# Block products of layer 0: copied accumulators in one two-bank tile, four weight loads in place of two

## The chip, the cores and the metric

One core of a Trainium2 chip runs the kernel. Its engines have queues of their own: PE (TensorE, matmul; PEld is its weight load), DVE (VectorE), ACT (ScalarE), POOL (GpSimd) and SP (SyncE), which here only issues DMAs. Data lie in SBUF, 128 partitions wide; matmuls write to PSUM, 8 banks of 128 x 512 float32. The metric is the device time of one execution in microseconds (us). Before the change the median of 3 runs was 2519.68 us (2517.79 to 2521.02).

## The reference

One inference step of a two-layer decoder. A prompt of 1024 tokens and 8 single-token samples share all weights, model width 1024. Each layer has a mixer, then a SwiGLU FFN, with norms and a residual around both. Only the FFN matters here:

```python
D_FF = ((8 * D_MODEL + 3 * 256 - 1) // (3 * 256)) * 256      # 2816

def swiglu(h, w_gu, w_down):
    gate, up = jnp.split(h @ w_gu, 2, axis=-1)
    return (jax.nn.silu(gate) * up) @ w_down
```

With `h` of 1024 columns, `h @ w_gu` has 2 x 2816 columns: 22 blocks ("columns", f = 0 to 21) of 128 for the gate and 22 for up.

## The kernel before

**Two groups.** The tokens are worked in two groups, g = 0 with 512 prompt tokens and g = 1 with 512 prompt tokens and the 8 samples (520, as two halves of 260). Everything is transposed: features on the partitions, tokens along the free axis.

**Split matmuls.** Float32 matmuls are made of three `float32r` ones. A raw weight block is copied by ACT to a rounded high part (L259, L561), DVE subtracts that for the low part (L260, L562), and PE multiplies high x high, high x low, low x high into one accumulator. The raw blocks come by DMA on SP into pool `wraw` (5 buffers, tile names w); the split parts lie in `wspl` (5 buffers, ws).

**Block products.** For group 1 some columns of the FFN are made by a seven-product scheme on 2 x 2 blocks in place of eight. The two token halves are one axis of blocks, gate and up another, and the two halves of the 1024 input features the third. A column's weights are four raw blocks of 512 x 128: a11 and a12 are the gate's upper and lower features, a21 and a22 those of up. `sums_here` loads them and gives, for product j, either a raw block or a sum: j = 1 needs a21 + a22, j = 2 needs kept3 = a11 + a21 and kept2 = kept3 + a22, j = 4 uses kept3 and j = 5 needs kept2 + a12. So four DVE sums a column (L536), seven ACT copies (L561) and seven DVE subtractions (L562). The token side's sums are made once by `sums_w` and reused in all columns.

`gate_up_w` runs the seven products (12 matmuls each, 84 a column, L571) on four accumulators. Their order, with what lies between:

- p0 into pa; L578: ACT writes -pa into pb
- p1 into pd; p2 onto pb; L581: ACT writes -pb into pc
- p3 onto pa; L584: silu of pa is one half of the gate
- p4 onto pb; L587: ACT copies pd; L589: DVE adds it to pb
- p5 onto pc; L591: DVE subtracts the copy of pd from pc
- p6 onto pb; L593: silu of the second half; L594 and L595: products of gate and up; then a split to the tile m that w_down reads.

**Where it is used.** Class `ffn` (layer 0) uses it for columns 10 to 21 of group 1: parts 2, 3 and 4 of the FFN in the `PARTS` of 5, 5, 4, 4 and 4 columns. Each part ends with 8 projections by `w_down` (L273) of that part's columns. Its accumulators come from `quads`: two tiles of two banks from pool `mmp` (2 buffers), pa and pd in the first, pb and pc in the second. Its raw blocks are two C tiles of two blocks each (`cpool`, 4 buffers of 128 x 2 x 512). The part before runs beside the stick-breaking and memory attention of group 0, whose last steps (scores L866, softmax, transposes L893, values L907) use the small banks `smp` (3 banks of 512, tile names s). Class `ffn_w` (layer 1) uses it for columns 4 to 21 of group 1, after `mmp` and `smp` were closed: eight single banks, four tags q0 to q3 of two buffers, so pa to pd of two columns have banks of their own. Its first block column (column 4) takes C tiles, later ones A tiles (`apool`, 8 buffers). Column 4 stands beside `store_y`, which transposes the first group's result (L1455), copies it to C tiles (L1458) and stores those (L1460), and beside `token_rows` (L483).

**The order.** The program is recorded by generators that `weave` interleaves by given weights; a scheduler then sets the order of each engine's instructions, and adds the waits, from its own estimates. A tile's buffer is reused when all readers of the tile that had it are done. The order of PE, DVE, ACT and SP below is that of the built program.

Of the kernel before, what the change touches and what calls it, by code (L numbers as in the profile page):

```python
# [8 lines left out]
F32 = mybir.dt.float32  # L9
# [8 lines left out]
P = 128  # L18
# [5 lines left out]
def tile_decoder(  # L24
# [12 lines left out]
    DFF = w_down.shape[1]  # L37
# [10 lines left out]
    def pool(name, bufs, **kw):  # L48
        return ctx.enter_context(tc.tile_pool(name=name, bufs=bufs, **kw))

    const = pool("const", 1)
    wraw = pool("wraw", 5)
    wspl = pool("wspl", 5)
    xpool = pool("xpool", 8)
    apool = pool("apool", 8)
# [8 lines left out]
    mmp = banks.enter_context(tc.tile_pool(name="mmp", bufs=2, space=PSUM))  # L64
# [6 lines left out]
    def nm(s):  # L71
        uid[0] += 1
        return f"{s}_{uid[0]}"
# [12 lines left out]
    def Q(i):  # L86
        return single[0].tile([P, 512], F32, tag=f"q{i}", name=nm("q"))
# [6 lines left out]
    def A(dt=F32):  # L94
        return apool.tile([P, 2, WID], dt, tag="a", name=nm("a"))
# [7 lines left out]
    def R_one():  # L103
        r = rpool.tile([P, ND, WID], F32, tag="r", name=nm("r"))
        return [r[:, k, :] for k in range(ND)]
# [5 lines left out]
    def C():  # L111
        return cpool.tile([P, 2, 512], F32, tag="c", name=nm("c"))

    def S():
        if single:
            turn[0] += 1
            return Q(3 * (turn[0] % 2))
        return smp.tile([P, 512], F32, tag="s", name=nm("s"))

    def small(shape, dt=F32, tag="sm", bufs=None):  # L120
        return spool.tile(shape, dt, tag=tag, name=nm(tag), bufs=bufs)
# [35 lines left out]
    for lv in range(7):  # L157
        m = 1 << lv
# [17 lines left out]
    def gcol(l, i, k):  # L176
        o = (l * 4 + i) * ND + k
        return par[:, o : o + 1]
# [64 lines left out]
    def pv(ps, g):  # L243
        return ps[:, 0, :G] if g == 0 else ps[:, :, : PW[1]]
# [62 lines left out]
    def sq_acc(acc, src, k, n):  # L307
        if k == 0:
            nc.scalar.activation(acc[:, :n], src, AF.Square)
        else:  # L310
            t = N()
            nc.scalar.activation(t[:, :n], src, AF.Square)  # L312
            nc.vector.tensor_add(acc[:, :n], acc[:, :n], t[:, :n])  # L313
# [207 lines left out]
        return mt, last  # L521

    def sums_here(l, f, raws, outs):
        cols = []
        for m0 in (f * P, DFF + f * P):
            r = raws()
            nc.sync.dma_start(
                r.rearrange("p a (k m) -> p (a k) m", m=P), w_gu[l][:, m0 : m0 + P].rearrange("(k p) m -> p k m", p=P)
            )
            cols.append(r)  # L530
        (a11, a12), (a21, a22) = ((r[:, 0, :], r[:, 1, :]) for r in cols)
        kept = {}

        def add(a, b):
            t = outs()
            nc.vector.tensor_add(t, a, b)  # L536
            return t

        def weight(j):
            if j == 1:  # L540
                return add(a21, a22)
            if j == 2:
                kept[3] = add(a11, a21)
                kept[2] = add(kept[3], a22)
                return kept[2]
            if j == 4:
                return kept[3]
            if j == 5:
                return add(kept[2], a12)
            return (a11, None, None, a12, None, None, a22)[j]  # L550

        return weight
# [51 lines left out]
    class ffn_w:  # L604
# [12 lines left out]

        def raws(self):
            if self.pi:
                return apool.tile([P, 2, 512], F32, tag="a", name=nm("w"))  # L620
            return C()

        def part(self, pi):
            l, n, h = self.l, NG[1], PW[1]
            f0, nf = PARTS[pi]
            last = pi == len(PARTS) - 1
            mids = []
            for j in range(nf):
                self.pi = pi
                if f0 + j < self.plain:  # L630
                    mt, ins = gate_up_q(l, f0 + j, self.x)
                    mids.append(mt)
                    with tc.issue_after(ins.ins):
                        for _ in range((1, 2, 1, 0)[j]):
                            next(self.sums, None)
                else:
                    mids.append(gate_up_w(
                        sums_here(l, f0 + j, self.raws, lambda: wraw.tile([P, 512], F32, tag="w", name=nm("w"))),
                        self.ops, self.spl, lambda: [Q(i) for i in range(4)]
                    )[0])  # L640
                yield
            if pi == 0:
                self.R = R_one()
            if last:
                self.acc = small([P, WID], tag="st", bufs=3)
                nc.scalar.preload_act_table_set("natural_log_exp_and_others")
            for m in range(ND):
                w = split_w(w_down[l], f0, nf, m * P)
                pp = [Q(2 * (m % 2) + a) for a in range(2)]
                for k in range(nf):  # L650
                    wh, wl = w[k]
                    for wi, (wt, xi) in enumerate(((wh, 0), (wh, 1), (wl, 0))):
                        for a in range(2):
                            nc.tensor.matmul(  # L654
                                pp[a][:, :h], wt, mids[k][:, xi, a * h : (a + 1) * h],
                                start=(k == 0 and wi == 0), stop=(k == nf - 1 and wi == 2),
                            )
                for a in range(2):
                    d = self.R[m][:, a * h : (a + 1) * h]
                    if pi == 0:  # L660
                        nc.scalar.copy(d, pp[a][:, :h])
                    else:
                        nc.vector.tensor_add(d, d, pp[a][:, :h])
                if last:
                    sq_acc(self.acc, self.R[m][:, :n], m, n)
                    nc.scalar.activation(self.R[m][:, :n], self.R[m][:, :n], AF.Copy, scale=gcol(l, 3, m))
                    if m == 3:
                        first_half(self)
                if m % 2:
                    yield  # L670
# [4 lines left out]
    class ffn:  # L675
        def __init__(self, g, l, xt, rows=False, prod=NF):
# [2 lines left out]
            self.ops = []  # L679
            self.sums = sums_w(xt, self.ops, lambda: A(F32R))  # L680

        def quads(self):
            ta, tb = (mmp.tile([P, 2, 512], F32, tag="mm", name=nm("mm")) for _ in range(2))
            return ta[:, 0, :], tb[:, 0, :], tb[:, 1, :], ta[:, 1, :]

        def part(self, pi):
            g, l = self.g, self.l
            n = NG[g]
            f0, nf = PARTS[pi]
            last = pi == len(PARTS) - 1  # L690
            mids = []
            for j in range(nf):
                if f0 + j >= self.prod:
                    mt, gate = gate_up_w(
                        sums_here(l, f0 + j, C, lambda: wraw.tile([P, 512], F32, tag="w", name=nm("w"))),
                        self.ops, lambda: wspl.tile([P, 2, 512], F32R, tag="ws", name=nm("ws")), self.quads,
                    )
                    mids.append(mt)
                    yield
                    continue  # L700
                pg = proj(g, w_gu[l], 0, ND, (f0 + j) * P, self.xt)
                sg = silu(None, pg, g)
                pu = proj(g, w_gu[l], 0, ND, DFF + (f0 + j) * P, self.xt)
                nc.vector.tensor_mul(sv(sg, g), sv(sg, g), pv(pu, g))  # L704
                mt = M(F32R)
                split_to((mt[:, 0, :n], mt[:, 1, :n]), sg[:, :n])
                mids.append(mt)
                yield
            if last and self.prod < NF:
                with tc.issue_after(gate.ins):  # L710
                    nc.scalar.preload_act_table_set("natural_log_exp_and_others")
            if pi == 0:
                self.R = R_one()
            if last:
                self.acc = small([P, WID], tag="st", bufs=3)
            for m in range(ND):
                ps = proj(g, w_down[l], f0, nf, m * P, mids)
                evac_raw(g, self.R, ps, m, self.acc, pi == 0, last)
                if last and self.rows:
                    nc.scalar.activation(  # L720
                        self.R[m][:, :n], self.R[m][:, :n], AF.Copy, scale=gcol(l, 3, m)
                    )
                    if m == 3:
                        first_half(self)
                if m % 2:
                    if f0 + nf == self.prod < NF:
                        next(self.sums, None)
                    yield
# [759 lines left out]
    f0 = ffn(0, 0, o0.x)  # L1488
# [28 lines left out]
    f0 = ffn(0, 1, o0.x)  # L1517
# [44 lines left out]
```

## Time and profile before

| | us |
|---|---|
| median of 3 runs | 2519.68 |
| profiled execution, its own time | 2518.8 |
| its span on the core | 2517.1 |
| PE busy | 2460.4 (98%) |
| PE weight loads busy | 2157.6 (86%) |
| DVE busy | 1670.4 (66%) |
| ACT busy | 1202.5 (48%) |

The profile is one execution taken by the hardware profiler. Its times are us from the start of the span unless marked ns. In a timeline a row is: start, length, engine and line, operation, output<-input by tile names, shape and count, and in brackets the idle time before it with what ended it. Rows that follow each other are merged, and an instruction's length overlaps the next one's start, so lengths of a merged row add up to more than the distance of starts. L571 is line 571 of the kernel, whatever calls it; the tile names tell the callers apart: mm and s are the layer-0 FFN's accumulators, q those of the last FFN. Matmuls are pipelined and their ends are modelled, and a few per cent of their records can be missing.

### The profile page before, as it was taken

To read this page: it belongs to the slowest core of one execution; us is meant where nothing else is said; L and a number is where in the kernel's file an instruction comes from. 1 tells how busy PE (TensorE), PEld (TensorE's weight loads), DVE (VectorE), ACT (ScalarE), POOL (GpSimd) and SP (SyncE) were. 2 spreads that over 40 slices of the span, in tenths; PEclk is the share of its full clock that TensorE was granted. 3 is DMA by queue.
4 is the path that set the end of the run, shared out by engine and by line. 5 is a ranking of instruction groups with operands and counts; after the bars stand their busy time and mean duration, and the time that the engine had idled before them with its cause. 6 is when DMAs were issued, how large, how long until landed. Compare 5 with 4: busy or idle time off the path is not lost. (4 is left out here: it accounts for less than half of the span.)

```text
span 2517.1 us, 40253 instructions
## 1 busy us (share of the span) xinstructions
PE 2460.4 (98%) x15421; PEld 2157.6 (86%) x15421; DVE 1670.4 (66%) x2972; ACT 1202.5 (48%) x2315; POOL 45.5 (2%) x59
## 2 busy tenths in 40 slices
PE   8999999999999999999999999999999999999998
PEld 6888988877877898999898889877787798999997
DVE  5766556654765576655866685777677548667775
ACT  5446543243433454555544554555454445454445
POOL 1000000000000000000000100021000000000000
PEclk9999999999999999999999999999999999999999
DMA  5352242233643447332232546544453244343332
GB/s 185 114 164 68 76 151 80 63 109 116 181 126 96 127 146 230 103 91 65 60 93 84 156 122 193 163 147 128 126 156 116 79 121 127 95 118 96 99 94 68
DMA packets 450634, 297.87 MB, mean 118 GB/s; under 512 B 16645, under 2 KB 413522, under 8 KB 450442
## 3 DMA queue, kind: packets, MB, share of 16 engines
q1 hardware_dynamic: 447882, 286.92, 37.9%
q0 software_dynamic: 2560, 8.39, 1.1%
q8 instruction: 121, 1.98, 0.3%
q14 instruction: 71, 0.58, 0.1%
HBM read 265.44 MB, written 29.80 MB: 117 GB/s over the span
## 5 line engine op out<-in xcount | busy, mean ns | idle before, releaser
L273 PE MATMUL mm<-x,ws 128*128 128x512 f32 (+1 forms) x6624 | 1193.6, 338 | 0.0
L273 PEld LDWEIGHTS mm<-x,ws 128*128 128x128 f32 x6624 | 1009.4, 188 | 152.3 <-issue 12.2
L259 ACT CAST ws<-w 128x512 fp32r<-128x512 f32 (+1 forms) x664 | 390.5, 589 | 665.4 <-PE mm L273 525.3
L260 DVE TENSOR_TENSOR ws<-w,ws 128x512 fp32r<-128x512 f32 (+1 forms) x664 | 428.8, 649 | 271.4 <-ACT ws L259 262.5
L273 PE MATMUL mm<-m,ws 128*128 128x512 f32 (+1 forms) x2112 | 394.6, 343 | 0.0
L273 PEld LDWEIGHTS mm<-m,ws 128*128 128x128 f32 x2112 | 324.6, 189 | 50.2 <-issue 2.5
L561 ACT CAST ws<-w 128x512 fp32r<-128x512 f32 x171 | 105.5, 621 | 85.4 <-PE q L654 25.1
L562 DVE TENSOR_TENSOR ws<-w,ws 128x512 fp32r<-128x512 f32 x171 | 116.9, 687 | 28.7 <-ACT ws L561 27.6
L654 PE MATMUL q<-m,ws 128*128 128x260 f32 x1056 | 129.1, 283 | 0.0
L654 PEld LDWEIGHTS q<-m,ws 128*128 128x128 f32 x1056 | 127.2, 188 | 0.7 <-ACT m L280 0.2
L571 PE MATMUL q<-y,ws 128*128 128x260 f32 x864 | 114.6, 285 | 3.7 <-DVE t L589 1.8
L571 PEld LDWEIGHTS q<-y,ws 128*128 128x128 f32 x864 | 108.7, 191 | 4.8 <-DVE t L589 2.5
L446 DVE TENSOR_TENSOR r<-r,mm 128x512 f32<-128x512 f32 (+1 forms) x96 | 65.9, 687 | 49.1 <-PE mm L273 48.3
L571 PE MATMUL mm<-a,ws 128*128 128x260 f32 x576 | 78.3, 288 | 17.9 <-ACT mm L578 16.1
L571 PEld LDWEIGHTS mm<-a,ws 128*128 128x128 f32 x576 | 71.7, 188 | 22.7 <-ACT mm L578 18.6
L290 DVE TENSOR_SCALAR t<-mm 128x512 f32<-128x512 f32 (+1 forms) x70 | 48.3, 690 | 61.7 <-PE mm L273 61.5
L571 PE MATMUL q<-x,ws 128*128 128x260 f32 x648 | 87.1, 283 | 1.5 <-ACT ws L561 1.4
L571 PEld LDWEIGHTS q<-x,ws 128*128 128x128 f32 x648 | 81.7, 189 | 2.0 <-ACT ws L561 1.6
L704 DVE TENSOR_TENSOR t<-t,mm 128x512 f32<-128x512 f32 (+1 forms) x54 | 37.1, 688 | 56.6 <-PE mm L273 55.9
L294 DVE TENSOR_TENSOR t<-t,t 128x512 f32<-128x512 f32 (+1 forms) x54 | 37.4, 692 | 53.9 <-ACT t L293 53.9
L313 DVE TENSOR_TENSOR st<-st,n 128x512 f32<-128x512 f32 (+1 forms) x98 | 67.0, 690 | 6.6 <-ACT n L312 5.0
L280 ACT CAST m<-t 128x512 fp32r<-128x512 f32 (+1 forms) x88 | 54.8, 623 | 20.2 <-DVE t L704 8.2
(355 smaller groups left out, 2873.0 us busy)
## 6 DMA issues: line engine op xcount, KB each, us to landing
w<-in_w_gu SPq DMA_DIRECT2D x232, 256.0 KB
w<-in_w_down SPq DMA_DIRECT2D x160, 256.0 KB
w<-in_w_in_a SPq DMA_DIRECT2D x80, 256.0 KB
w<-in_w_gu SPq DMA_DIRECT2D x34, 512.0 KB
w<-in_w_o SPq DMA_DIRECT2D x64, 256.0 KB
c<-in_w_gu SPq DMA_DIRECT2D x26, 512.0 KB
w<-in_w_mem_kv SPq DMA_DIRECT2D x32, 256.0 KB
c<-in_cache_mem_k SPq DMA_DIRECT2D x16, 512.0 KB
```

What stands on the lines that cost most here:

```text
L259: nc.scalar.copy(ws[:, 0, :n, :], raw[:, :n, :])
L260: nc.vector.tensor_sub(ws[:, 1, :n, :], raw[:, :n, :], ws[:, 0, :n, :].bitcast(F32))
L273: nc.tensor.matmul(ps[:, a, : PW[g]], wt, xt[k][:, xi, o : o + PW[g]], start=(k == 0 and wi == 0), stop=(k == nk - 1 and wi == 2),)
L280: nc.scalar.copy(dst[0], src)
L290: nc.vector.tensor_scalar(sv(x, g), pv(ps, g), -44.0, None, op0=ALU.max)
L294: nc.vector.tensor_mul(d, d, x[:, :n])
L313: nc.vector.tensor_add(acc[:, :n], acc[:, :n], t[:, :n])
L446: nc.vector.tensor_add(dst, dst, pv(ps, g))
L561: nc.scalar.copy(w[:, 0, :], src)
L562: nc.vector.tensor_sub(w[:, 1, :], src, w[:, 0, :].bitcast(F32))
L571: nc.tensor.matmul(ps[:, :h], w[:, wj, k * P : (k + 1) * P], x[:, xi, :], start=(first and k == 0 and wi == 0), stop=(k == 3 and wi == 2), ...
L654: nc.tensor.matmul(pp[a][:, :h], wt, mids[k][:, xi, a * h : (a + 1) * h], start=(k == 0 and wi == 0), stop=(k == nf - 1 and wi == 2),)
```

## The change

Four things change, all in the block products.

1. `ffn.quads` takes one two-bank tile from `mmp` for pb and pc, and two small banks from `smp` for pa and pd.
2. `sums_here` loads the four raw blocks by four DMAs of 256 KB in the order a11, a21, a12, a22, in place of two DMAs of 512 KB (gate, then up).
3. `raws` gives four views: in `ffn` the halves of two C tiles as before, in `ffn_w` the halves of two A tiles as before, but for column 4 of `ffn_w` four buffers of `wraw` in place of two C tiles.
4. The sums go to work tiles `B` (`bpool`, 7 buffers of 128 x 512, used by the attention and by `sums_w`) in place of `wraw` buffers.

```diff
     def sums_here(l, f, raws, outs):
-        cols = []
-        for m0 in (f * P, DFF + f * P):
-            r = raws()
+        a11, a12, a21, a22 = raws()
+        for r, k0, m0 in (
+            (a11, 0, f * P), (a21, 0, DFF + f * P), (a12, 512, f * P), (a22, 512, DFF + f * P),
+        ):
             nc.sync.dma_start(
-                r.rearrange("p a (k m) -> p (a k) m", m=P), w_gu[l][:, m0 : m0 + P].rearrange("(k p) m -> p k m", p=P)
-            )
-            cols.append(r)
-        (a11, a12), (a21, a22) = ((r[:, 0, :], r[:, 1, :]) for r in cols)
+                r.rearrange("p (k m) -> p k m", m=P), w_gu[l][k0 : k0 + 512, m0 : m0 + P].rearrange("(k p) m -> p k m", p=P)
+            )
...
         def raws(self):                                  # ffn_w
             if self.pi:
-                return apool.tile([P, 2, 512], F32, tag="a", name=nm("w"))
-            return C()
+                ts = [apool.tile([P, 2, 512], F32, tag="a", name=nm("w")) for _ in range(2)]
+                return [t[:, a, :] for t in ts for a in range(2)]
+            return [wraw.tile([P, 512], F32, tag="w", name=nm("w")) for _ in range(4)]
...
-                        sums_here(l, f0 + j, self.raws, lambda: wraw.tile([P, 512], F32, tag="w", name=nm("w"))),
+                        sums_here(l, f0 + j, self.raws, B),
...
+        def raws(self):                                  # ffn
+            ts = [C(), C()]
+            return [t[:, a, :] for t in ts for a in range(2)]
+
         def quads(self):
-            ta, tb = (mmp.tile([P, 2, 512], F32, tag="mm", name=nm("mm")) for _ in range(2))
-            return ta[:, 0, :], tb[:, 0, :], tb[:, 1, :], ta[:, 1, :]
+            t = mmp.tile([P, 2, 512], F32, tag="mm", name=nm("mm"))
+            return S(), t[:, 0, :], t[:, 1, :], S()
...
-                        sums_here(l, f0 + j, C, lambda: wraw.tile([P, 512], F32, tag="w", name=nm("w"))),
+                        sums_here(l, f0 + j, self.raws, B),
```

## The prediction

> **What bounds the kernel now.** I read the page first (busy times), then PE's waits in the stage that the change touches, then PE's timeline there and in the last FFN, then the busy times by stage, and last DVE, ACT and SP around the gaps. A product is one gate/up column f; its seven block products are p0 to p6, a prime marks the next column, and f10 is column 10.
>
> The page:
>
> ```profile
> span 2517.1 us, 40253 instructions
> PE 2460.4 (98%) x15421; PEld 2157.6 (86%) x15421; DVE 1670.4 (66%) x2972; ACT 1202.5 (48%) x2315; POOL 45.5 (2%) x59
> ```
>
> PE is the bound, so only time in which PE stands still can be won. PE's own waits from 1200 to 1480 us, where the layer-0 block products run (columns 10 to 21 of the second group), as us in total, times, longest:
>
> ```profile
> PE mm L571 <- ACT mm L578: 16.1, 12, 1.7
> PE mm L571 <- DVE t L591: 1.4, 2, 1.3
> PE mm L571 <- DVE t L589: 1.2, 1, 1.2
> ```
>
> All twelve columns wait for L578, the copy of -pa into pb. One column of that stage in PE's timeline, then the same column's length in the last FFN, where each accumulator has its own bank:
>
> ```profile
> 1254.90 3.17 PE L571 MATMUL mm<-a,ws 128*128 128x260 f32 x24 [1.72 <-ACT mm L578]
> 1257.90 1.61 PE L571 MATMUL mm<-x,ws 128*128 128x260 f32 x12
> 1259.35 1.60 PE L571 MATMUL mm<-a,ws 128*128 128x260 f32 x12
> 1260.79 3.23 PE L571 MATMUL mm<-x,ws 128*128 128x260 f32 x24
> 1264.07 1.71 PE L571 MATMUL mm<-a,ws 128*128 128x260 f32 x12
> 1267.48 3.17 PE L571 MATMUL mm<-a,ws 128*128 128x260 f32 x24 [1.70 <-ACT mm L578]
> ...
> 2240.11 3.04 PE L571 MATMUL q<-y,ws 128*128 128x260 f32 x24
> 2250.22 3.04 PE L571 MATMUL q<-y,ws 128*128 128x260 f32 x24
> ```
>
> The first column takes 1267.48 - 1254.90 = 12.58 us, the second 2250.22 - 2240.11 = 10.11 us, for the same 84 matmuls. The 24 at 1254.90 are p1 and p2, then come p3, p4, then p0' around p5 (24), then p6, and then PE stands until L578 is done. The wait's chain, on DVE and ACT:
>
> ```profile
> 1266.08 0.41 DVE L594 TENSOR_TENSOR t<-t,mm 128x260 f32<-128x260 f32 x1
> 1267.05 0.37 ACT L578 ACTIVATE mm<-mm 128x260 f32<-128x260 f32 x1
> ```
>
> p6 ends, DVE reads pb for the last time (L594), only then may L578 write pb' into the same two-bank tile, and p1' waits for L578 because it writes pd in the tile whose other bank L578 reads. Busy time by stage (us; busy and count of PE, PEld, DVE, ACT, POOL; clock; DMA share; GB/s): columns 10-13, 14-17, 18-21 of that FFN, then 10-13 and 14-17 of the last FFN, then its column 4:
>
> ```profile
> 1235.49:1290.55 55.06, 47.99 (x363) 44.90 (x362) 37.33 (x69) 28.46 (x61) 0.00 (x0) 1.00 0.47 134
> 1312.30:1363.79 51.49, 44.76 (x352) 42.57 (x351) 32.27 (x57) 24.63 (x51) 0.00 (x0) 1.00 0.43 123
> 1385.55:1435.79 50.24, 44.75 (x352) 42.62 (x350) 31.97 (x56) 25.61 (x52) 7.88 (x8) 1.00 0.54 167
> 2307.75:2348.12 40.37, 40.37 (x338) 40.37 (x337) 30.79 (x55) 24.08 (x50) 0.00 (x0) 1.00 0.45 131
> 2172.35:2194.46 22.11, 17.28 (x126) 15.86 (x125) 12.86 (x24) 12.12 (x26) 0.00 (x0) 0.92 0.52 158
> ```
>
> The fourth row is PE without a gap: 40.37 / 338 = 0.1194 us a matmul. At that pace the others need 43.3, 42.0, 42.0 and 15.0 us, so PE stands for 11.7, 9.5, 8.2 and 7.1 us: 36.5 us in all that this change can reach.
>
> **The change, part by part.**
>
> *Banks (quads).* pa and pd go to two of the three small banks; pb and pc keep one two-bank tile, and the two such tiles now alternate from column to column. L578' writes a tile whose last reader was two columns ago, so it need not wait for L594, and p1' shares no tile with L578'. What is late next: p5 still writes pc in the tile where DVE's L589 reads pb, and p6 waits for L591. In the changed build's instruction order PE has p0' and two matmuls of p1' between p4 and p5 (14 x 0.1194 = 1.7 us) and seven of p1' between p5 and p6 (0.8 us). In the rows above those covers were nine matmuls and three; the pair 1260.79 to 1264.07 took 3.28 us for 24 x 0.1194 = 2.87, so 0.4 us were lost there, and 0.6 and 0.5 us more cover should hide it. DVE, busy 30.79 of 40.37 us in the last FFN with the same sums and splits, can hold PE's full pace; there it has more weight buffers than the five here. I leave 0.15 us a column: 0.6 us in each group of four. Saved: columns 14-17 9.5 - 0.6 = 8.9 us, 18-21 8.2 - 0.6 = 7.6 us. Bounds: all of it (17.7), or 1.23 us still lost per column to L589 (the row at 1249.24 below), 17.7 - 8 x 1.23 = 7.9. I take the value near the upper end, since the last FFN's rows are the same work with the banks apart.
>
> Columns 10-13 start beside the end of the memory attention, which also lives in the three small banks:
>
> ```profile
> 1235.49 0.71 PE L571 MATMUL mm<-x,ws 128*128 128x260 f32 x3
> 1236.30 1.13 PE L907 MATMUL s<-b,c 128*128 128x256 f32 x4
> ...
> 1240.52 0.30 PE L893 MATMUL s<-ident,b 128*128 128x128 f32 x1
> ...
> 1249.24 2.08 PE L571 MATMUL mm<-x,ws 128*128 128x260 f32 x15 [1.23 <-DVE t L589]
> ```
>
> Today p0 starts at 1235.49 and fills the time until the turned weights at 1240.52. In the changed order p0's bank is that of the last scores, so p0 comes behind the first of those transposes, and PE has nothing else until the softmax is done. With nothing between its steps I put that at about 1238.5 (estimate; bounds 1237.4, the end of the row at 1236.30, and 1240.5, today's place), so some 2 to 3 us are lost at once. p1 and p2 also need the sums that now sit behind the attention's last DVE work. The gaps of columns 11-13 go as above. Of the 11.7 us I keep 4.7: 7.0 saved (bounds 4 and 9).
>
> *Sums to work tiles (B, seven) and four loads in place of two.* No arithmetic is added: the instruction counts of PE, DVE and ACT stay the same, only SP issues 60 more DMAs.
>
> ```profile
> L527 SPq DMA_DIRECT2D w<-in_w_gu x34: 367/368/3337, 2212.1 to 2445.8; - x34
> L527 SPq DMA_DIRECT2D c<-in_w_gu x26: 367/368/1030, 991.3 to 2175.5; - x26
> ```
>
> 60 x 0.368 = 22 us of SP's time over 30 columns, 0.74 us a column of 10.1: hidden by SP's slack, if no load is due within that. How much slack a load has shows where the buffer is freed (the split of a22), and where the sum that needs the next load in it stands:
>
> ```profile
> 1244.67 0.69 DVE L562 TENSOR_TENSOR ws<-c,ws 128x512 fp32r<-128x512 f32 x1
> ...
> 1248.16 0.69 DVE L536 TENSOR_TENSOR w<-c 128x512 f32<-128x512 f32 x1 [2.20 <-DMA c<-in_w_gu]
> ...
> 1257.35 0.69 DVE L562 TENSOR_TENSOR ws<-c,ws 128x512 fp32r<-128x512 f32 x1 [1.57 <-ACT ws L561]
> ...
> 1262.31 0.68 DVE L536 TENSOR_TENSOR w<-c 128x512 f32<-128x512 f32 x1
> ```
>
> From 1245.36 to 1248.16, a 512 KB load took 2.8 us with its wait. A column later the buffer is free at 1258.04, the load would be there at 1260.84, and is used at 1262.31: 1.47 us of slack. The one more issue on SP (0.37) fits. Cost: nothing; if the cover is gone, up to 2.8 - 1.47 = 1.3 us a column (rival 2). A gain is not excluded, as half a load releases p0 earlier; PE shows no wait for p0's weights here, so I count none. With the sums out of the five raw buffers, loads of w_down start earlier; PE has no gap there, so nothing follows. [...]
>
> *Column 4 of the last FFN.* Its two 512 KB loads went to C tiles, which the storing of y also uses; now four raw buffers hold them:
>
> ```profile
> 2172.35 1.91 PE L1455 MATMUL q<-ident,r 128*128 128x128 f32 x16
> 2175.65 0.51 PE L571 MATMUL q<-x,ws 128*128 128x260 f32 x2 [1.38 <-ACT ws L561]
> ...
> 2182.49 0.51 PE L571 MATMUL q<-y,ws 128*128 128x260 f32 x2 [1.57 <-ACT ws L561]
> ...
> 2174.19 1.26 SPq L1460 DMA_DIRECT2D out_y_prompt<-c  x2
> 2175.51 0.46 SPq L527 DMA_DIRECT2D c<-in_w_gu  x1
> ...
> 2181.09 0.69 DVE L536 TENSOR_TENSOR w<-c 128x512 f32<-128x512 f32 x1 [4.77 <-DMA c<-in_w_gu]
> ```
>
> The second load is issued at 2175.51, behind two stores of y, and DVE waits for it until 2181.09. In the changed order all four loads stand ahead of the stores on SP, five splits stand ahead of the store's copies on ACT, and PE runs p0 to p6 in one piece with the transposes behind them. Of the 7.1 us idle I keep 1.1 for the banks of those transposes: 6.0 saved (bounds 3 and 7.1).
>
> **Sum.** 8.9 + 7.6 + 7.0 + 6.0 = 29.5 us; less 1 us for the odd new wait in columns 5-21 of the last FFN: 28.5. The profiled execution took 2518.8 us (span 2517.1), 0.9 under the median of 2519.68: 2518.8 - 28.5 + 0.9 = 2491.
>
> **Rivals.** 0.2% of the time, 5 us, is about what a measurement tells from no change.
>
> 1. *DVE becomes the next wait.* p5 and p6 wait for L589 and L591, which stand behind sums and splits in DVE's queue. At 1.23 us in each of 12 columns it costs 12 x (1.23 - 0.15) = 13 us: 2504. For: by its row lengths DVE has 9.2 us of work in a column of 10.1, end to end (seven splits and four sums of 0.69, four of 0.41), less where they overlap. Against: the last FFN holds the pace.
> 2. *The halves land late (the other side).* The sum a21+a22 for two columns ahead stands on DVE just before L591, so a late load holds DVE, and p6 and p1' behind it. At 1.3 us in all 30 columns: 39 us, 2491 + 39 = 2530, slower; it decides from 28.5 / 30 = 0.95 us a column. Against: 1.47 us of slack, DMA share 0.5. A mild form, 0.5 us a column (under half of 1.3), gives 15 us: 2506. [...]
> 3. *The change doesn't do what it says:* the wait for L578 only moves from p1' to p2', as when pb' found no free tile. Then only column 4 gains: 2513, or nothing, 2519. Against: two tiles, one used a column.
>
> **How the numbers follow.** Forecast 0.70; rival 1 0.14 (2504); rival 2 mild 0.07 (2506) and full 0.05; rival 3 0.04. Faster: 0.70 + 0.14 + 0.07 = 0.91; same 0.04; slower 0.05. The range goes from all 36.5 us won (2483) to the mild rivals, 2506, and leaves out 0.09 and a little of each edge.
>
> **What would show it.** In the profile after: no PE wait for L578 in that stage, columns 14-17 at about 42.6 us for 352 matmuls (now 51.49), 18-21 alike, columns 10-13 about 48, a new PE wait for the softmax at their start, column 4 with its 22.11 us down to about 16. Wrong it would be if PE's rows there show waits for L589, L591 or the splits of 1 us a column, or DVE's sums wait for loads in most columns.

## Result, and the profile after

The changed kernel takes 2500.99 us (median of 6 runs, 2498.41 to 2503.64) against 2519.24 us (6 runs) for the kernel before: ratio 0.9928, 95% interval 0.9915 to 0.9940. It is faster by 18.3 us, where 28.5 had been forecast; 2500.99 lies inside the range, 10 us above the point. The profiled execution took 2501.9 us. Its page:

```profile
span 2500.2 us, 40342 instructions
PE 2457.2 (98%) x15421; PEld 2156.9 (86%) x15421; DVE 1669.7 (67%) x2972; ACT 1202.1 (48%) x2315; POOL 46.6 (2%) x59
```

In the changed kernel the line numbers of the block products shift by one: the load is L528, the sums L535, the splits L560 and L561, the block matmul L570, the copies -pa and -pb L577 and L580, the addition to pb L588, the subtraction from pc L590, the two products of gate and up L593 and L594. The softmax's transposes are L897. PE's waits from 1200 to 1480 us (us in total, times, longest):

```profile
PE s L897 <- DVE b L887: 1.5, 1, 1.5
PE mm L570 <- DVE t L590: 1.3, 1, 1.3
PE mm L570 <- DVE t L588: 0.6, 1, 0.6
PE s L570 <- DVE ws L561: 0.5, 1, 0.5
```

The twelve waits for the copy of -pa (16.1 us) are gone, and the softmax wait that was forecast for the start is there. Busy time by stage, columns as in the prediction: columns 10-13 (from the same place of the stage as there; p0 itself now starts at 1239.18), 14-17, 18-21 of layer 0, then column 4 of the last FFN:

```profile
1236.24:1285.91 49.67, 46.96 (x365) 44.55 (x363) 43.95 (x80) 30.12 (x64) 0.00 (x0) 1.00 0.42 122
1307.67:1353.02 45.35, 43.82 (x353) 42.44 (x352) 34.98 (x62) 24.51 (x51) 0.00 (x0) 1.00 0.38 111
1374.79:1418.12 43.33, 43.33 (x351) 42.36 (x350) 31.19 (x55) 25.57 (x52) 7.86 (x8) 1.00 0.51 165
2154.52:2168.89 14.37, 14.37 (x126) 14.37 (x125) 9.59 (x19) 9.50 (x21) 0.00 (x0) 1.00 0.42 143
```

They were 55.06, 51.49, 50.24 and 22.11 us. To compare kernels whose columns begin at other places I use three longer stretches, whose ends are the same instructions in all: the block stage of layer 0 (from the first `w_down` projection after column 9 to the first one of the next projection phase), column 4 of the last FFN with what lies around it (from `store_y`'s first transpose to the token rows' L493), and the rest, to the end of the span. Before:

```profile
1195.63:1457.35 261.72, 242.38 (x1898) 232.75 (x1897) 185.01 (x345) 121.48 (x255) 7.88 (x8) 1.00 0.33 98
2172.35:2211.67 39.32, 34.49 (x270) 32.94 (x269) 17.86 (x33) 20.67 (x47) 0.00 (x0) 0.96 0.44 134
2211.67:2517.10 305.43, 292.74 (x2424) 289.83 (x2421) 214.68 (x397) 152.66 (x304) 0.00 (x0) 0.98 0.32 96
```

And after:

```profile
1196.40:1439.67 243.27, 238.76 (x1898) 231.76 (x1897) 184.02 (x345) 121.46 (x255) 7.86 (x8) 1.00 0.35 105
2154.52:2186.11 31.59, 31.59 (x270) 31.46 (x269) 12.84 (x26) 18.24 (x43) 0.00 (x0) 1.00 0.40 132
2186.11:2500.20 314.09, 295.83 (x2424) 291.76 (x2421) 215.07 (x397) 152.84 (x304) 0.00 (x0) 0.98 0.32 93
```

Layer 0 won 18.45 us, column 4 won 7.73, and the rest of the last FFN, columns 5 to 21, *lost* 8.66: 17.5 us, and the span fell by 16.9. The loss begins in column 5. Its DVE rows, after:

```profile
2203.97 0.68 DVE L561 TENSOR_TENSOR ws<-w,ws 128x512 fp32r<-128x512 f32 x1
2208.28 0.69 DVE L535 TENSOR_TENSOR b<-w 128x512 f32<-128x512 f32 x1 [3.63 <-DMA w<-in_w_gu]
...
2212.50 0.69 DVE L561 TENSOR_TENSOR ws<-b,ws 128x512 fp32r<-128x512 f32 x1
2213.11 0.42 DVE L588 TENSOR_TENSOR t<-t,q 128x260 f32<-128x260 f32 x1
```

and PE's:

```profile
2208.67 1.61 PE L570 MATMUL q<-x,ws 128*128 128x260 f32 x12
2213.58 2.35 PE L570 MATMUL q<-y,ws 128*128 128x260 f32 x12 [3.30 <-DVE t L588]
```

DVE waits 3.63 us for a load of column 7, because the sum a21 + a22 of column 7 stands in its queue ahead of L588 of column 5. Then the four sums and four splits of column 7 follow back to back, and only at 2213.11 L588, for which PE has stood 3.30 us. The 12 matmuls behind the gap take 2.35 us where the row before has 1.61: PE's granted clock is 0.50 there, from 2214.36 to 2217.77.

### The profile page after: what moved, and what is told of

Read it like the earlier page. It is cut to its first block, busy times and chain, and to the rows that moved or that the text cites. A ratio compares the mean times of both kernels' runs of the same rounds, so it can differ in the third digit from the quotient of the medians.

```text
span 2500.2 us, 40342 instructions
## 1 busy us (share of the span) xinstructions
PE 2457.2 (98%) x15421; PEld 2156.9 (86%) x15421; DVE 1669.7 (67%) x2972; ACT 1202.1 (48%) x2315; POOL 46.6 (2%) x59
## 4 chain that ended last, share of the span: by engine, by line
PE 89%; DVE 5%; DMA 2%; ACT 2%; issue 1%; POOL 0%; SPq 0%; DVEq 0%; ACTq 0%
PE mm L273 58%; PE q L570 5%; PE q L654 5%; PE s L1188 2%; PE q L509 2%; PE mm L1056 2%; PE mm L570 2%; PE s L570 1%; PE s L911 1%; PE s L1344 1%; PE s L870 1%; DVE b L535 1%; PE mm L820 1%; PE ns L965 1%; PE mm L847 1%
## 5 line engine op out<-in xcount | busy, mean ns | idle before, releaser
L570 PE MATMUL q<-y,ws 128*128 128x260 f32 x864 | 114.3, 285 | 7.2 <-DVE t L588 7.1
L570 PEld LDWEIGHTS q<-y,ws 128*128 128x128 f32 x864 | 107.7, 189 | 9.2 <-DVE t L588 9.2
L560 ACT CAST ws<-b 128x512 fp32r<-128x512 f32 x120 | 74.4, 621 | 57.3 <-PE q L654 15.7
L561 DVE TENSOR_TENSOR ws<-b,ws 128x512 fp32r<-128x512 f32 x120 | 82.4, 688 | 22.9 <-ACT ws L560 21.4
L570 PE MATMUL q<-x,ws 128*128 128x260 f32 x648 | 87.7, 285 | 0.0
L570 PEld LDWEIGHTS q<-x,ws 128*128 128x128 f32 x648 | 82.7, 191 | 0.0
L281 DVE TENSOR_TENSOR m<-t,m 128x512 fp32r<-128x512 f32 (+1 forms) x88 | 60.8, 691 | 1.5 <-ACT m L280 0.7
L570 PE MATMUL mm<-a,ws 128*128 128x260 f32 x432 | 59.0, 285 | 1.7 <-DVE t L590 1.3
```

Of the source, the lines that this page charges most:

```text
L281: nc.vector.tensor_sub(dst[1], src, dst[0].bitcast(F32))
L560: nc.scalar.copy(w[:, 0, :], src)
L561: nc.vector.tensor_sub(w[:, 1, :], src, w[:, 0, :].bitcast(F32))
L570: nc.tensor.matmul(ps[:, :h], w[:, wj, k * P : (k + 1) * P], x[:, xi, :], start=(first and k == 0 and wi == 0), stop=(k == 3 and wi == 2), ...
```

## Experiments

The theories for the missing 10 us: *splitting* (a column's loads land later as four halves than as two), *SP's order* (with the sums in B, loads of `w_down` move ahead of column 7's on SP), and *DVE's queue* (its in-order sums and splits hold L588 and L590, in layer 0 too). Kernels with two load forms have the lines of the block products shifted by 8 more: there the whole load is L527, the sums L543, the splits L568 and L569, the block matmul L578, the copy of -pa L585, the addition L596 and the subtraction L598. The softmax's transposes are L903 there.

**Whole loads.** The changed kernel with two 512 KB loads a column, except column 4 of the last FFN:

```diff
-        a11, a12, a21, a22 = raws()                    # four loads of 256 KB
+        ts = raws()
+        if len(ts) == 2:                               # C or A tiles
+            for r, m0 in zip(ts, (f * P, DFF + f * P)):
+                nc.sync.dma_start(r.rearrange("p a (k m) -> p (a k) m", m=P), w_gu[l][:, m0 : m0 + P]...)
+            a11, a12, a21, a22 = (r[:, a, :] for r in ts for a in range(2))
+        else:                                          # column 4: four, as changed
```

> The changed kernel with its two 512 KB loads per column again (gate, then up) in the C and A tiles; column 4 of the last FFN keeps its four raw buffers and four loads, banks and B tiles stay. Three theories for the 10 us that the change brought less than forecast. Splitting (a column's four half loads land later than two whole ones did): the 0.5 us per column that layer 0 still loses (about 5 us) and the 8.7 us that columns 5 to 21 of the last FFN lost both go, about 2489. SP's order (with the sums in B the raw buffers are free earlier, so w_down loads stand ahead of column 7's loads on SP, and DVE's sum for column 7 comes late): the order is still so here, so the 3.3 us wait for L588 in column 5 stays, about 2500, or 2496 if layer 0 alone gains. DVE's queue (sums and splits are the limit): nothing changes, about 2501.

Measured: 2496.82 us (2491.84 to 2499.24), ratio 0.9908 (0.9891 to 0.9925). Layer 0 and the rest of the last FFN:

```profile
1195.53:1437.73 242.20, 238.49 (x1898) 231.68 (x1897) 183.99 (x345) 121.45 (x255) 7.83 (x8) 1.00 0.35 105
2186.95:2497.50 310.55, 295.48 (x2424) 291.57 (x2421) 215.07 (x397) 152.90 (x304) 0.00 (x0) 0.98 0.32 94
```

In this profile 3.5 us of the loss go with the splitting, 5.1 stay, and layer 0 moves by only 1.1. None of the three answers alone. The four executions lie between 2491.84 and 2499.24, and the profiled one is the slowest of them.

**Banks alone.** The kernel before with the new `quads` of layer 0 and nothing else:

```diff
-            ta, tb = (mmp.tile([P, 2, 512], F32, tag="mm", name=nm("mm")) for _ in range(2))
-            return ta[:, 0, :], tb[:, 0, :], tb[:, 1, :], ta[:, 1, :]
+            t = mmp.tile([P, 2, 512], F32, tag="mm", name=nm("mm"))
+            return S(), t[:, 0, :], t[:, 1, :], S()
```

> The kernel before with the banks alone (quads of layer 0): two 512 KB loads, sums in the raw buffers, column 4 in C tiles. Its gain is what the banks bring in columns 10 to 21 of layer 0. By splitting or by SP's order: the 23.5 us of the forecast (8.9 + 7.6 + 7.0), about 2495.5. By DVE's queue: as much as the changed kernel shows there, 18.4 us, about 2501. The last FFN should be as in the kernel before: column 4 with 22 us.

Measured: 2501.24 us (2498.12 to 2504.53), ratio 0.9933 (0.9916 to 0.9949). The time is the one that DVE's queue gave, but by luck, as the rows show. Layer 0, and 3.4 us of the last FFN's column 5:

```profile
1195.97:1437.66 241.69, 237.83 (x1898) 231.70 (x1897) 184.84 (x345) 121.53 (x255) 7.87 (x8) 1.00 0.36 106
2218.20:2221.60 3.40, 3.40 (x16) 3.40 (x17) 2.51 (x6) 0.89 (x2) 0.00 (x0) 0.50 0.57 161
```

The banks bring 20.0 us in layer 0 with the loads as before, so neither splitting nor the order of loads explains why it was not 23.5. Nor does DVE's queue explain much of it: PE waits here 0.8 us for L589 in all, once, and 2.5 and 0.5 us beside the softmax; in columns 14 to 21 it has no wait (43.43 and 43.22 us for the two groups of four). The second row stands behind a PE gap of 1.97 us: the granted clock is 0.50, and 16 matmuls take 3.40 us in place of 16 x 0.1194 = 1.9, which costs 1.5 us. The rest of its last FFN took 307.3 us, 1.9 more than before the change, though loads and sums are as there; why the gap was 1.97 and not 1.28 us in this profile stays open.

**Sums back in the raw buffers.** The changed kernel, halves kept, with one edit at both calls of `sums_here`:

```diff
-    sums_here(l, f0 + j, self.raws, B),
+    sums_here(l, f0 + j, self.raws, lambda: wraw.tile([P, 512], F32, tag="w", name=nm("w"))),
```

> The changed kernel with the sums back in the raw buffers wraw; half loads, banks and column 4 as changed. SP's order is then again that of the kernel before in the last FFN: column 7's loads stand ahead of the first w_down loads. By SP's order: the wait of DVE's sum for column 7's load (3.6 us), PE's 3.3 us for L588 and the half clock behind it (some 1.6 us) go, and columns 5 to 21 win most of the 8.7 us back, about 2493. By splitting: the loads stay late, waits of 1 us or more for L588 stay, about 2500. By DVE's queue: 2501.

Measured: 2495.23 us (2494.03 to 2496.75), ratio 0.9907 (0.9890 to 0.9923).

**Banks and column 4 alone.** The last edit and the whole loads together; against the kernel before only the banks and this are left:

```diff
         def raws(self):                                  # ffn_w
...
-            return C()                                   # column 4, two 512 KB loads
+            return [wraw.tile([P, 512], F32, tag="w", name=nm("w")) for _ in range(4)]
```

> Banks and column 4's four raw buffers alone: two 512 KB loads for all other columns, sums in the raw buffers. By splitting and by SP's order alike: all 28.5 us of the forecast, about 2491 or a little under; by DVE's queue: layer 0 as in the changed kernel, but if DVE also sets the last FFN, no better than 2500. Against the banks alone this run gives column 4's price: 7.7 us by the changed kernel's trace, if nothing behind it gives it back.

Measured: 2492.18 us (2491.26 to 2493.61), ratio 0.9895 (0.9878 to 0.9911). The rest of the last FFN, first with the sums back and halves:

```profile
2185.84:2495.00 309.16, 294.90 (x2424) 291.84 (x2421) 214.85 (x397) 152.88 (x304) 0.00 (x0) 0.98 0.32 95
```

then with the sums back and whole loads:

```profile
1196.68:1440.37 243.69, 239.61 (x1898) 233.03 (x1897) 185.16 (x345) 121.72 (x255) 7.87 (x8) 0.99 0.35 105
2186.69:2491.90 305.21, 293.60 (x2424) 290.42 (x2421) 214.78 (x397) 152.47 (x304) 0.00 (x0) 0.98 0.33 96
```

Against the banks alone the raw buffers of column 4 bring 9.1 us by the times (2501.24 to 2492.18); the stretch of column 4 itself gives 7.5 (39.13 to 31.60). The four cells of loads and place of the sums are 305.2 (whole, raw buffers: as before the change), 309.2 (halves, raw buffers), 310.6 (whole, B) and 314.1 (halves, B). So halves cost 4.0 and 3.5 us, B 5.3 and 4.9, and they add. The times have the same order: 2492.2, 2495.2, 2496.8, 2501.0, which gives 3.0 and 4.2 for halves, 4.6 and 5.8 for B. Each cell is one profile, and the banks alone, with the loads and sums of the first cell, took 307.3, so some 2 us of a cell can be chance; of the ratios only the first and the last have intervals that don't overlap.

The two costs fall in different places. With the sums in the raw buffers, the last matmul of column 6 starts 40.24 us into the stretch with halves and 36.88 with whole loads, and from there to the end the distance stays at 3.2 to 3.4 us: halves cost once, around the end of column 5. With the sums in B the loss goes on in later columns.

How halves cost, in the last load that column 7's sum waits for. With whole loads, its issue on SP and the sum on DVE:

```profile
2203.08 0.37 SPq L527 DMA_DIRECT2D w<-in_w_gu  x1
2207.02 0.69 DVE L543 TENSOR_TENSOR w<-w 128x512 f32<-128x512 f32 x1 [2.16 <-DMA w<-in_w_gu]
```

with halves, sums in the raw buffers:

```profile
2203.09 0.51 SPq L528 DMA_DIRECT2D w<-in_w_gu  x1
2208.08 0.69 DVE L535 TENSOR_TENSOR w<-w 128x512 f32<-128x512 f32 x1 [3.62 <-DMA w<-in_w_gu]
```

The half is used 4.99 us after its issue, the whole load 3.94 us after (4.56 in the kernel with whole loads and sums in B, 2203.55 to 2208.11). In the whole-load kernel PE's gap in column 5 is 1.11 us and the clock stays; with halves it is 3.01 and a granted clock of 0.50 follows: 1.9 us of gap and some 1.5 us of clock are the whole cost. Why the half lands later isn't shown. SP's order is the same in these two, and column 5 is late in one only. With the sums in B four loads of `w_down` do stand ahead of column 7's on SP, but its last half is issued 17.2 us into the stretch in either order (2203.29 in the changed kernel, 2203.09 here). So the theory of SP's order falls as the cause of column 5.

How B costs, in column 13 of the last FFN. DVE in the changed kernel:

```profile
2321.93 0.69 DVE L535 TENSOR_TENSOR b<-w 128x512 f32<-128x512 f32 x1 [1.73 <-DMA w<-in_w_gu]
...
2325.07 0.68 DVE L535 TENSOR_TENSOR b<-b,w 128x512 f32<-128x512 f32 x1
...
2326.27 0.42 DVE L588 TENSOR_TENSOR t<-t,q 128x260 f32<-128x260 f32 x1
```

and with the sums in the raw buffers (the rows are 2.7 us nearer to the start of the stretch):

```profile
2322.67 0.69 DVE L260 TENSOR_TENSOR ws<-w,ws 128x512 fp32r<-128x512 f32 x1 [1.10 <-ACT ws L259]
2323.28 0.42 DVE L588 TENSOR_TENSOR t<-t,q 128x260 f32<-128x260 f32 x1
2323.61 0.69 DVE L535 TENSOR_TENSOR w<-w 128x512 f32<-128x512 f32 x1
```

With the sums in work tiles the scheduler has set all four sums of the next block column ahead of L588; with the five raw buffers, which `w_down` uses too, one sum stands there, and behind L588. The place of the sums is the only edit between the two kernels. In the first order a load that is 1.73 us late holds L588, and PE waits 1.01 us for it. From 2120 us on DVE's sums wait 14 times for loads (19.0 us) in the changed kernel, 7 times (11.9 us) with the sums back.

**Without the sums.**

```diff
         def weight(j):
-            if j == 1: return add(a21, a22)
-            ...                                        # kept3, kept2, j = 4, j = 5
-            return (a11, None, None, a12, None, None, a22)[j]
+            return (a11, a21, a22, a12, a21, a12, a22)[j]
```

> The changed kernel without the four DVE sums of each column: products 1, 2, 4 and 5 take raw blocks (a21, a22, a21, a12) in place of sums, so the values of these columns are not the reference's; all loads, splits and matmuls stay. Column 7's sum waits 3.6 us for its load in the changed kernel, ahead of L588, L590 of the column before. If the loss in the last FFN reaches PE only through sums that stand in DVE's queue ahead of L588 and L590, the time after column 4 falls from 314.1 us to the 305 of the kernel before: about 2492. If the late loads hold ACT's splits and PE as much without the sums, it stays at 314: 2501. For layer 0: if DVE's work of sums and splits sets the pace, its block stage (243.3 us from the first w_down projection to the end of the FFN) falls by another 5 us, to 238; if not, it stays within 1.5 us of 243.

Measured: 2486.52 us (2485.53 to 2487.10), ratio 0.9878 (0.9861 to 0.9894). Layer 0, its columns 18-21 and the rest of the last FFN:

```profile
1193.12:1432.94 239.82, 238.04 (x1898) 231.67 (x1897) 157.57 (x297) 122.35 (x255) 9.39 (x8) 1.00 0.36 106
1367.94:1411.38 43.44, 43.44 (x351) 42.37 (x350) 27.07 (x47) 25.77 (x52) 9.39 (x8) 1.00 0.51 161
2180.82:2483.80 302.98, 293.09 (x2424) 290.85 (x2421) 177.26 (x329) 152.45 (x304) 0.00 (x0) 0.98 0.33 97
```

Halves and column 4 are as in the changed kernel, and ACT waits once 4.0 us for a half load, but PE has no wait in any block column of the last FFN: 303.0 us, 11.1 less than the changed kernel. So in these profiles the loss there reaches PE only through sums in DVE's queue. The run takes away the sums' work (some 2.8 us of DVE a column) together with their waits for loads, and doesn't tell the two apart; it ends 2.45 us below the kernel before, and 1.2 of the 11.1 us is a shorter wait at the transposes of the result at the end (2.3 to 1.1). Layer 0 falls by 3.45 us, between the two values expected. Of that, 1.9 us lie in columns 14-17 (45.35 to 43.46) and 1.7 up to the end of columns 10-13; columns 18-21 take 43.44 us without the sums and 43.33 with them, so there DVE's queue costs nothing. PE's wait for the softmax at the start, 1.7 us, stays.

**Sums on POOL.** Banks and column 4 alone, and in `add`:

```diff
-            nc.vector.tensor_add(t, a, b)
+            nc.gpsimd.tensor_add(t, a, b)
```

> Banks and column 4's raw buffers alone (two 512 KB loads, sums in the raw buffers, 2492 us), with the four sums of a column on POOL in place of DVE. If DVE's in-order queue is what a late load holds, PE's waits for L588 and L590 go and layer 0 and the last FFN win some 2 to 5 us: 2487 to 2490. If POOL's sum takes so long that the raw buffers or product 1 wait for it (a column has 10.1 us for four sums, three of them in a chain), the columns become longer than 10.6 us and the time goes above 2497.

Measured: 2512.32 us (2510.54 to 2517.02), ratio 0.9975 (0.9965 to 0.9985); worse than on DVE by 20 us. The stretch of layer 0:

```profile
1195.90:1446.36 250.46, 243.18 (x1898) 234.16 (x1897) 183.03 (x297) 119.76 (x255) 76.00 (x56) 0.99 0.35 102
```

and the largest of POOL's groups (busy us, mean ns, then its idle time):

```profile
L543 POOL TENSOR_TENSOR w<-w,w 128x512 f32<-128x512 f32 x55 | 84.5, 1537 | 449.4 <-DVE ws L260 420.9 <-DVE ws L569 19.0 <-issue 4.9
```

A sum takes 1.54 us there, 0.69 on DVE. The four of a column are 6 us of POOL, and three depend on each other. Against the same kernel with the sums on DVE, layer 0 is 6.8 us longer (250.46 against 243.69), column 4's stretch 4.5 (36.06 against 31.60) and the rest 8.9 (314.08 against 305.21). What exactly is late next I did not isolate.

**Column 10 on two-bank tiles.** Banks and column 4 alone, but the first block column of layer 0 keeps the accumulators of before:

```diff
         def quads(self):
+            if self.first:
+                self.first = False
+                ta, tb = (mmp.tile([P, 2, 512], F32, tag="mm", name=nm("mm")) for _ in range(2))
+                return ta[:, 0, :], tb[:, 0, :], tb[:, 1, :], ta[:, 1, :]
```

> Banks and column 4's raw buffers alone (2492 us), but column 10, the first block column of layer 0, keeps both its accumulator tiles in the two-bank pool as in the kernel before; columns 11 to 21 have the changed banks. In the changed kernels PE stands 1.5 to 2.5 us for the softmax at the start of column 10, since p0's bank is one of the attention's three small ones, and in two of four profiles the granted clock fell to 0.5 for 3.4 us right behind that gap. If the shared small bank is the cause, p0 fills the gap again: the wait for the transposes goes, columns 10 to 13 win 2.5 to 4 us, about 2489. If column 10 then waits for L578 as before (1.7 us once or twice), the gain is 1 us or less, 2491 to 2492.

Measured: 2490.25 us (2485.27 to 2493.14), ratio 0.9888 (0.9872 to 0.9905). Layer 0:

```profile
1196.53:1436.16 239.63, 238.23 (x1898) 231.97 (x1897) 184.90 (x345) 121.25 (x255) 7.85 (x8) 1.00 0.36 106
```

4.1 us less than in the profile without it. By the times it is 1.9 us less, which can't be told from nothing. PE at the start of column 10, first with the shared small bank:

```profile
1241.01 0.33 PE L903 MATMUL s<-ident,b 128*128 128x128 f32 x1 [2.52 <-DVE b L893]
```

then with the two-bank tiles (L922 is the values' matmul, L907 before):

```profile
1236.39 0.71 PE L578 MATMUL mm<-x,ws 128*128 128x260 f32 x3
1237.21 1.13 PE L922 MATMUL s<-b,c 128*128 128x256 f32 x4
1237.99 1.43 PE L578 MATMUL mm<-x,ws 128*128 128x260 f32 x9
1239.88 1.72 PE L578 MATMUL mm<-a,ws 128*128 128x260 f32 x12 [0.46 <-ACT mm L585]
```

p0 fills the gap again; the wait for the copy comes back with 0.46 us. Some 2 of the 4.1 us are the granted clock of 0.50 that followed the gap in the profile without this: the banks alone, where the same gap wasn't followed by it, took 241.69.

**Up first.** The same, with the load of up issued first and into the buffer that comes free first:

```diff
-            for r, m0 in zip(ts, (f * P, DFF + f * P)):
+            for r, m0 in zip(ts, (DFF + f * P, f * P)):
...
-            a11, a12, a21, a22 = (r[:, a, :] for r in ts for a in range(2))
+            a21, a22, a11, a12 = (r[:, a, :] for r in ts for a in range(2))
```

> The kernel with whole loads, sums in the raw buffers and column 10 on two-bank tiles (2490 us), with the load of up (a21, a22) issued ahead of that of the gate, so that it takes the buffer that comes free first. In the profile without this, column 7's two loads were issued 3.0 us apart (2200.1 and 2203.1) and DVE's sum a21 + a22 waited 2.2 us for the second. If the sum's wait for its load is what still delays L588 and L590 in the last FFN, the first wait of column 5 and DVE's 11 us of waits for these loads shrink, and the time falls by 1 to 3 us, to 2487 to 2489. If the gate's block a11, now the later one, is then what ACT's split for product 0 waits for, nothing is won or a few us are lost: 2490 to 2495.

Measured: 2489.03 us (2488.55 to 2490.53), ratio 0.9889 (0.9872 to 0.9905): no difference that can be told. The rest of the last FFN, and PE in column 5:

```profile
2183.89:2488.80 304.91, 293.21 (x2424) 290.35 (x2421) 214.48 (x397) 153.00 (x304) 0.00 (x0) 0.98 0.32 96
```

```profile
2208.38 1.70 PE L578 MATMUL q<-y,ws 128*128 128x260 f32 x12 [0.33 <-DVE t L596]
```

Column 5's gap shrank from 1.56 us to 0.33, but DVE's sums wait longer for loads in all (16.8 us against 11.5), and later columns give it back: a miss. The fastest kernels of this study are this one and the one before it: ratios 0.9889 and 0.9888 to the kernel before the change, against 0.9928 for the changed kernel, about 10 us further down.

## Why the prediction was right, and where it was not

- **Direction and mechanism of the banks: right.** All twelve waits for the copy of -pa went. Columns 18-21 gave 6.9 us (forecast 7.6), columns 14-17 6.1 (8.9), columns 10-13 5.4 (7.0). The stretch won 18.45 where 23.5 were forecast.
- **"I leave 0.15 us a column": too little, and mostly for another reason than DVE.** Columns 18-21 take 43.33 us with PE at work throughout, and 43.44 without the sums, so no wait is left there. What was off is the pace behind "at that pace the others need 43.3, 42.0, 42.0": 0.1194 us a matmul was read in the last FFN. In layer 0 the 349 matmuls from p0 to the last p6 take 0.124 each, as around the first matmul of p5 and of p6 a matmul's distance to the next is some 0.2 us in place of 0.12, with and without the sums; why stays open. That is 0.7 us in columns 18-21 and, by the banks alone (43.43 us), 0.8 in 14-17. The cover was misread too: in the profile after, eight matmuls run between p4 and p5 (from 1382.01) and six between p5 and p6 (from 1384.60), not 14 and seven.
- **Rival 1, DVE as the next wait, holds in part.** In columns 14-17 a late half load for the next columns holds the sum, and p6 waits 1.29 us for L590 (0.99 with whole loads and sums in B): there the sums in B cost as in the last FFN (the distance from the end of columns 10-13 to that of columns 14-17 is 67.1 and 66.9 us with B, 65.2 to 66.3 in the three profiles with the sums in the raw buffers).
- **Columns 10-13, "some 2 to 3 us are lost at once": right.** p0 starts at 1239.18, which is 1238.4 in the times of the profile before, where the stage began 0.77 us earlier (estimate 1238.5). The loss can be avoided: with column 10 on two-bank tiles the stage is 2 us shorter than in the banks alone, and 4.1 shorter where the gap had lowered the clock.
- **Column 4, 6.0 us: it gave 7.7.** PE has no gap left in it (14.37 us busy of 14.37), so the 1.1 us kept for the transposes' banks were not needed.
- **"Less 1 us for the odd new wait in columns 5-21": the step that failed;** it is 8.66 us. Of the 11 us that the stretches miss of the forecast it is the largest part (7.7; layer 0 missed 5.1, and column 4 gave 1.7 more). Two sentences carried it. "The one more issue on SP (0.37) fits. Cost: nothing" took two half loads to land like a whole one; the last half was used 4.99 us after its issue against 3.94. And "loads of w_down start earlier; PE has no gap there, so nothing follows" looked at the raw buffers that the move of the sums frees, but not at the sums: they move forward in DVE's queue, ahead of L588 and L590. The last FFN had its own row in the trace of before, DVE's waits for these loads (us in total, times, longest), which I did not cost:

```profile
DVE w L536 <- DMA w<-in_w_gu: 11.1, 8, 3.1
```

- **The 1.47 us of slack were misread.** The load used at 1248.16 was not issued when the buffer came free at 1245.36, but before it, and the next one at 1258.07:

```profile
1243.23 0.37 SPq L527 DMA_DIRECT2D c<-in_w_gu  x1
1258.07 0.37 SPq L527 DMA_DIRECT2D c<-in_w_gu  x1
```

So the first was used 4.93 us after its issue, not 2.8, and the second at 1262.31, 4.24 us after. By its semaphore's updates in the trace of before the second landed 3.73 us after its issue (3.77 in the median of the 24 loads of layer 0), which leaves some 0.5 us. By that, halves had little cover in layer 0 either; they cost 0.5 to 1.1 us there (243.69 to 244.20 and 242.20 to 243.27).
- **Rival 2 was the right mechanism** (a late load holds DVE's sum, and that holds p6 and p1'), but in columns 5-21 of the last FFN. 8.66 / 17 = 0.51 us a column is its mild price by luck: the loss comes in uneven steps (the stretch up to the end of column 6 lost 3.5 of the 8.66, 1.5 of it by the clock), and halves and the place of the sums share it. Its layer-0 part stayed small. The sign that the prediction named, "DVE's sums wait for loads in most columns", is there in the last FFN: 14 waits (19.0 us) for 18 columns, 8 (11.1 us) before; in layer 0 there are six (3.5 us) for 12. For the last half of column 7, 4.99 - 3.94 = 1.05 us more from issue to use was measured. The mean share of the DMA engines was 0.32 in the rest of the last FFN, and splitting cost 4.0 and 3.5 us there all the same: the sum needs the last half, and DVE waited 3.62 us for it.
- **Rival 3: excluded,** no wait took the copy's place.

## What to carry to other kernels

Freeing a buffer lets a scheduler move its writer forward: before calling such a move free, read what stands behind the moved instruction on its in-order engine, and what it can now wait for. Cost a change of loads at the place with the least slack among all callers, not at the one where the change was aimed. When two edits are bundled, try each without the other: here halves and work tiles cost 3 to 6 us each inside a change that gained 18. And a pace read in one stage need not hold in another: count what a stage takes when nothing waits.

## Hardware that I had not expected

- **The granted clock was halved behind some short PE gaps and not behind others.** In column 5 of the last FFN gaps of 0.33 (up first), 1.11 (banks and column 4 alone), 1.28 (before) and 1.56 us (column 10 on two-bank tiles) left the granted clock at 1.00; gaps of 1.97 (banks alone), 2.29 (whole loads), 3.01 (sums back) and 3.30 us (the changed kernel) were followed by 0.50 for 3.41 us, which cost some 1.5 us (in the banks alone 16 matmuls took 3.40 us in place of 1.9). It isn't the length alone: in column 4 before the change a clock of 0.50 (2183.49 to 2186.90) followed gaps of at most 1.57 us, and the same 2.52 us gap at the start of column 10 was followed by 0.50 in two profiles and by 1.00 in a third. In each profile the slow stretches begin whole multiples of 3.413 us apart (in the banks alone at 2163.61 and 2218.23, 16 times). Cut at that beat, the stretch ahead of the slow one and the slow one itself (sums back and halves, column 10), then the two that share the gap in the third profile (banks alone; the next one, to 1245.42, ran at 1.00 as well):

```profile
1237.41:1240.82 3.41, 0.89 (x8) 0.70 (x7) 2.34 (x7) 1.02 (x4) 0.00 (x0) 1.00 0.91 266
1240.82:1244.23 3.41, 3.41 (x14) 3.05 (x13) 1.99 (x3) 0.67 (x2) 0.00 (x0) 0.50 0.12 35
...
1235.19:1238.60 3.41, 2.12 (x10) 1.21 (x8) 3.41 (x8) 2.00 (x5) 0.00 (x0) 1.00 0.29 82
1238.60:1242.01 3.41, 1.73 (x13) 1.56 (x14) 1.31 (x5) 1.61 (x5) 0.00 (x0) 1.00 0.81 226
```

In the block stages of layer 0 and the last FFN up to 2440 us, over all ten profiles, ten of the eleven slow stretches follow a stretch of the beat with 0.60 to 1.61 us of PE work, and the eleventh one with 1.80; no stretch with less than 1.70 us was followed by full clock. Elsewhere one with 1.50 us was (1873.34 in the profile of the banks and column 4 alone), so it is no sharp limit. Nor does every slow stretch stand behind a gap: in the changed kernel 0.50 from 579.37 to 582.78 (from 579.23 before) follows a stretch with 3.41 us of PE work by the profile. What sets the clock, the traces don't show.
- **An issue right behind another took SP longer.** In the changed kernel a half load that is issued alone takes SP 0.37 us, one right behind another 0.51 in the median (63 of the 120). It isn't the size: whole loads take 0.37 alone, too, and the few issued in a row took 0.46 to 3.34 us before the change (8 of 60).
